# A hybrid decoder block on one core: the attention stage issued from a schedule made inside the kernel, with the last query tile and the first output products moved to the fourth and fifth query blocks

## The chip, the core and the metric

One core of one Trainium2 chip runs the whole kernel in one launch. The metric is the device time of an execution in microseconds (us). Before the change it is 1889.48 us, the median of three runs (1889.11 to 1890.73). The engines are named as in the profile: PE (TensorE, matrix products), PEld (its weight loads, which run beside the products), DVE (VectorE), ACT (ScalarE), POOL (GpSimd) and SP (SyncE, which here issues DMA transfers). "SPq" is the instruction queue of SP. Each engine takes its instructions strictly in the order in which they stand in its own program.

## The reference, cut to what matters

The block computes, on 1024 tokens of width 1024 in float32, a feed-forward part, a mixer and a second feed-forward part, each added to the running rows:

```python
h = h + 0.5 * swiglu(rms_norm(h, ffn1_norm[l]), ffn1_w_gu[l], ffn1_w_down[l])
h = h + hybrid_mixer(rms_norm(h, mix_norm[l]), w_in[l], ...)
h = h + 0.5 * swiglu(rms_norm(h, ffn2_norm[l]), ffn2_w_gu[l], ffn2_w_down[l])
return rms_norm(h, final_norm)
```

The change lies in the mixer. Half of its width is an attention of 8 query heads in 2 groups, with three branches that share the queries: compressed keys, selected key blocks and a window of 512 keys. With 16 blocks of 64 keys and 16 to be selected, every block is selected, so that the selected branch is plain causal attention. Each branch has its own softmax with a linear penalty on distance, and a gate from a sigmoid. The other half of the width is a gated linear recurrence, whose result is multiplied by a gate. Both halves together go through `w_out`.

## The kernel before

**Exact products from split operands.** Every float32 operand of a product is split into a high and a low part (`split`, lines 182 to 189: a copy on ACT or POOL, a subtraction on DVE), and `mm3` (lines 191 to 195) issues three products of 512 columns for one: high by high, high by low, low by high.

**The attention stage** (lines 1697 to 1768) runs from about 919 to 1249 us of the profiled execution. It goes over 8 blocks of 128 queries (`qb`), for each over the 2 groups (`g`), and for each group over its 4 heads (`hh`); `half` is 0 for the blocks 0 to 3 and 1 for 4 to 7. Below, (4,0) is block 4, group 0, and (4,0,2) its head 2. The steps of one head and one group are these:

- `att_soft`, lines 1261 to 1349: the scores of a head against the keys (`ka` high, `kl` low) are products on PE into a bank `a` (lines 1287 and 1288, 64 to 512 columns). DVE adds the distance table and finds the extreme (line 1295). The inner function `rest` then issues the exponentials on ACT (line 1333), the reciprocals of their sums on DVE (line 1336 for heads 0 and 1 together, line 1339 for heads 2 and 3) and the scaling on POOL (line 1345).
- `att_pv`, lines 1351 to 1396: for each block of keys, PE turns the four heads' probabilities with four transposes of 128 columns into a bank `b` (line 1376); ACT copies the high part `ph` (line 1378), DVE makes the low part `pt` (line 1379), and PE multiplies both with the values (line 1367) into the bank `o`. There are two banks `b`. The generator of one group is advanced while the scores of the next group are issued.
- Filling: a chain of generators `dense` is advanced between the heads. It holds work that is not attention: query projections (`att_proj_q`, lines 1181 to 1204; a tile of 128 columns of the query weights gives two heads and is 24 products of 512 columns), the gates of the recurrence (`late_gates`, lines 901 to 922: four times 24 products, a copy `ge` on ACT, and after the last one four sigmoids on ACT in a row) and, from block 4 on, the output product of the first 512 tokens (`wout`, lines 1399 to 1414).

**The filling before.** For the second half the query tiles go in the order 3, 0, the gates, then 1 and 2; at (3,1,2) the whole rest of that chain is issued, and only then the pool of the query weights is closed and the keys of the second half for group 0 are written (`att_kv`, lines 1237 to 1259, called in line 1722). Their high part `ka` lies in the buffer `wh` of the pool `wf`, which holds the weights of query tile 2 until that tile is done. The output product starts after the scores of (4,0): line 1745 makes its generator, and one step is issued at each head from (4,1) to (7,1), 28 steps in all. A step is half of a piece of 128 tokens by 256 columns: 12 products of 256 columns (lines 815 to 817). There are 16 pieces, so 32 steps; the last four are issued behind the last head (line 1750). Four pieces share one quarter of `w_out`, eight tiles of 256 KB (`wpages`, lines 370 to 380, tag `qa`, which the query heads use too). The step order within a piece is `kt` 0 to 3, which need the attention's result, then 4 to 7, which need the recurrence's result (lines 808 to 819). Behind the stage's last group, output products of the other 512 tokens (`rows_out`, lines 1757 to 1767; PE rows with `wq` as the moving operand and 512 columns) are issued between the parts of the last `att_pv`.

**What sets the order.** The code is written out as a straight program; the tile framework orders the instructions of every engine by the order of writing and by its own estimate of when each can start. `ordered` (lines 161 to 175) is a context that instead fixes, on each engine, the order in which the instructions were issued inside it. It is used at the kernel's start, and within `late_gates` for the four sigmoids. The attention stage as a whole is not in such a context.

## Time and profile before

| what | value |
|---|---|
| runs | 1889.11, 1889.48, 1890.73 us |
| profiled execution | 1889.76 us, its span 1888.0 us |
| PE, DVE, ACT, POOL busy in the span | 1863.8, 1348.6, 795.0, 535.0 us |
| granted TensorE clock | 0.999 |
| attention stage, first to last transpose | 934.9 to 1243.9 us |
| transposes, value products, output products of lines 815 to 817 with `wq` | 592, 296, 384 |
| ACT table loads, each 1283 ns | 9 in the program, 3 of them in the attention stage |

The page lists the busy time of each engine; a second view gives it by stretches of the span, a third the waits of one engine on another, and the timeline shows instructions in order of time. A PE product is counted busy from its start to a modelled end, so the products of a dense stream overlap: a product of 512 columns counts 0.38 us and the next one starts 0.21 to 0.22 us after it. A PE that counts as busy can therefore still be held up for a short while.

### The profile page before, as it was taken

What the parts mean: (1) busy time and instruction counts of PE and PEld (TensorE: products, weight loads), DVE (VectorE), ACT (ScalarE), POOL (GpSimd) and SP (SyncE); (2) the same over time, 40 slices, a digit from 0 to 9 for tenths busy, and PEclk for the clock granted to TensorE, in tenths of its full rate; (3) what the DMA queues carried; (4) which work ended last, traced back from release to release, by engine and by line L of the source; (5) the groups of instructions that cost most, each with busy time, mean ns of one, the idle gap of its engine ahead of it and who ended that gap; (6) DMA issues with size and microseconds to landing.
All of it is one profiled execution on the core that took longest, in us unless ns stands there. A gap on an engine that the chain in (4) does not pass through costs nothing.

```text
span 1888.0 us, 31252 instructions
## 1 busy us (share of the span) xinstructions
PE 1863.8 (99%) x11054; PEld 1620.8 (86%) x11054; DVE 1348.6 (71%) x2595; ACT 795.0 (42%) x1675; POOL 535.0 (28%) x641
## 2 busy tenths in 40 slices
PE   9999999999999999999999999999999999999998
PEld 6888888888888888889887888888888888888887
DVE  5988878657776545777477988737877776568686
ACT  5533333323323413334578777646333333323233
POOL 3132332324442001112345543311212222123222
PEclk9999999999999999999999999999999999999999
DMA  5246666428775232554522022553556675158664
GB/s 201 97 137 225 221 216 225 138 99 320 234 252 173 81 104 100 185 190 151 167 90 68 18 88 73 171 196 112 163 172 220 221 234 190 62 202 285 201 211 154
DMA packets 167260, 313.75 MB, mean 166 GB/s; under 512 B 17952, under 2 KB 50752, under 8 KB 167104
## 3 DMA queue, kind: packets, MB, share of 16 engines
q1 hardware_dynamic: 157568, 295.22, 47.2%
q10 hardware_dynamic: 9536, 16.53, 2.5%
q8 instruction: 87, 1.43, 0.3%
q14 instruction: 69, 0.57, 0.1%
HBM read 218.89 MB, written 92.80 MB: 165 GB/s over the span
## 4 chain that ended last, share of the span: by engine, by line
PE 87%; DVE 7%; ACT 3%; issue 2%; DMA 1%; POOL 1%; SPq 0%; POOLq 0%; ACTq 0%; DVEq 0%
PE b L193 18%; PE b L195 18%; PE b L194 18%; PE b L746 6%; PE b L744 6%; PE b L745 6%; PE b L1376 3%; PE b L1367 2%; PE b L969 1%; PE b L815 1%; ACT P L1333 1%; PE b L817 1%; PE b L816 1%; PE b L1288 1%; ACT ph L1378 1%
## 5 line engine op out<-in xcount | busy, mean ns | idle before, releaser
L193 PE MATMUL b<-xT,wp 128*128 128x512 f32 x1196 | 454.3, 380 | 1.7 <-DVE pd L696 1.3
L194 PE MATMUL b<-xT,wp 128*128 128x512 f32 x1196 | 453.8, 379 | 1.7 <-DVE xT L433 1.6
L195 PE MATMUL b<-xT,wp 128*128 128x512 f32 x1196 | 453.3, 379 | 0.0
L189 DVE TENSOR_TENSOR dw<-dr,dw 128x512 fp32r<-128x512 f32 x308 | 227.6, 788 | 62.1 <-ACT dw L187 51.0
L193 PEld LDWEIGHTS b<-xT,wp 128*128 128x128 f32 x1196 | 226.1, 189 | 37.0 <-DVE pd L696 1.7
L194 PEld LDWEIGHTS b<-xT,wp 128*128 128x128 f32 x1196 | 226.1, 189 | 35.4 <-DVE xT L433 3.5
L195 PEld LDWEIGHTS b<-xT,wp 128*128 128x128 f32 x1196 | 226.1, 189 | 32.7 <-DVE wp L189 0.3
L744 PE MATMUL b<-dw,dw 128*128 128x512 f32 x616 | 233.8, 380 | 0.3 <-DVE dw L189 0.3
L746 PE MATMUL b<-dw,dw 128*128 128x512 f32 x616 | 233.9, 380 | 0.0
L745 PE MATMUL b<-dw,dw 128*128 128x512 f32 x616 | 233.5, 379 | 0.0
L185 POOL TENSOR_SCALAR dw<-dr 128x512 fp32r<-128x512 f32 x154 | 127.2, 834 | 242.3 <-PE b L746 109.4
L187 ACT ACTIVATE wp<-ws 128x512 fp32r<-128x512 f32 x148 | 92.9, 629 | 235.5 <-PE b L194 226.1
L1345 POOL TENSOR_SCALAR P<-P,sm,gate 128x64 f32<-128x64 f32 (+8 forms) x192 | 126.8, 678 | 151.4 <-DVE sm L1336 54.0
L187 ACT ACTIVATE dw<-dr 128x512 fp32r<-128x512 f32 x154 | 91.8, 624 | 181.8 <-PE b L744 80.8
L189 DVE TENSOR_TENSOR wp<-ws,wp 128x512 fp32r<-128x512 f32 x148 | 113.8, 770 | 32.3 <-ACT wp L187 32.1
L187 ACT ACTIVATE wp<-wr 128x512 fp32r<-128x512 f32 x115 | 72.0, 627 | 145.7 <-PE b L194 120.8
L746 PEld LDWEIGHTS b<-dw,dw 128*128 128x128 f32 x616 | 116.4, 189 | 17.4 <-DVE dw L189 1.0
L744 PEld LDWEIGHTS b<-dw,dw 128*128 128x128 f32 x616 | 116.4, 189 | 17.2 <-issue 0.7
L745 PEld LDWEIGHTS b<-dw,dw 128*128 128x128 f32 x616 | 116.4, 189 | 16.3
L1333 ACT ACTIVATE P<-P,sm 128x64 f32<-128x64 f32 (+7 forms) x192 | 114.9, 600 | 35.4 <-DVE sm L1295 34.5
L529 POOL TENSOR_TENSOR ws<-wr 128x512 f32<-128x512 f32 x37 | 52.1, 1408 | 270.5 <-DVE wp L189 226.2
L193 PE MATMUL b<-xT,wh 128*128 128x512 f32 x320 | 125.8, 394 | 1.6 <-issue 1.4
(316 smaller groups left out, 3563.5 us busy)
## 6 DMA issues: line engine op xcount, KB each, us to landing
dr<-hs SPq DMA_DIRECT2D x242, 256.0 KB, 3.7
wr<-in_ffn_w_gu_dram SPq DMA_DIRECT2D x82, 512.0 KB, 4.2
hs<-hk SPq DMA_DIRECT2D x140, 256.0 KB, 4.0
hs<-wd SPq DMA_DIRECT2D x88, 256.0 KB, 3.1
wd<-in_ffn_w_down_dram SPq DMA_DIRECT2D x84, 256.0 KB, 3.4
dr<-in_ffn_w_down_dram SPq DMA_DIRECT2D x62, 256.0 KB, 4.4
wq<-wo SPq DMA_DIRECT2D x44, 256.0 KB, 3.3
wo<-wo SPq DMA_DIRECT2D x16, 512.0 KB, 2.7
```

The lines of the kernel that those rows point to most:

```text
L185: nc.gpsimd.tensor_scalar(out=hi, in0=src, scalar1=1.0, scalar2=1.0, op0=OP.mult, op1=OP.mult)
L187: nc.scalar.activation(out=hi, in_=src, func=AF.Copy)
L189: eng.tensor_tensor(out=lo, in0=src, in1=hi.bitcast(F32), op=OP.subtract)
L193: mm(ps, wh, xh, start=first, stop=False, skip_group_check=skip)
L194: mm(ps, wh, xl, start=False, stop=False, skip_group_check=skip)
L195: mm(ps, wl, xh, start=False, stop=last, skip_group_check=skip)
L744: mm(bs[t][:], hl[:, c], dh, start=first, stop=False, skip_group_check=True)
L745: mm(bs[t][:], hh[:, c], dh, start=False, stop=False, skip_group_check=True)
L746: mm(bs[t][:], hh[:, c], dl, start=False, stop=last, skip_group_check=True)
L1333: nc.scalar.activation(out=rng[br], in_=rng[br], func=AF.Exp, scale=-1.0, bias=m, accum_out=st[:, 6 + br:7 + br])
L1345: nc.gpsimd.tensor_scalar(out=rng[br], in0=rng[br], scalar1=st[:, 6 + br:7 + br], scalar2=self.gate[:, qb, h * 3 + br:h * 3 + br + 1], op0 ...
L1376: nc.tensor.transpose(b[:w, hh * 128:hh * 128 + 128], Ps[hh][i][:, c:c + w], self.ident[:])
```

## The change

**A planner.** A new class `Plan` stands in for the instruction builder inside a context `planned`. Calls to the five engines are recorded with the tiles that they read and write. `issue` then makes a schedule: it walks through time, keeps for each engine when it is free, for each operation when its inputs are ready, and for each tag when a buffer or a bank comes free, and takes next the operation that can start first, the earliest written one among equals. Durations come from formulas in `cost`. The operations are then issued for real in the order of their planned start, inside `ordered`, so that the order on every engine is the plan's. A function of ACT other than a copy carries its name, and a change of that function adds a table load of 1283 ns to the start that the plan sees. The whole loop of the attention stage, and what is written behind it up to the end of the last `att_pv`, goes through the plan. `flush("wq")` issues the plan up to the last operation that uses the pool of the query weights, so that the pool can be closed; the rest is planned again with that beginning held.

**The filling.** Query tile 2 of the second half leaves the chain that is used up at (3,1,2) and becomes a chain of its own: two steps at each of the heads (3,1,2) and (3,1,3), two at (4,0,0), three at (4,0,1), and what is left at (4,0,2). There the output product now starts, with two steps at each of the heads (4,0,2) and (4,0,3), then one at each head up to (7,1): 4 and 28, which is all 32. Within a piece the step with `kt` 4 to 7 now comes first.

**Buffers.** The keys of the second half for group 0 (`ka` and `kl`) lie in the pool `k1`, those for group 1 in the pool `wf`, in the buffers `wh` and `wl` of the query weights. In the first half, query tile 3 uses the bank `w` and not `b`, and in the second half tile 3 uses `b` and not `w`.

No instruction of the computation is added or left out. The program of ACT has 11 table loads in place of 9. The change moves all rows of the stage to line 208, the line in `issue` that calls the recorded operation.

The core of the diff:

```diff
+class Plan:
+    def cost(self, e, what, kw, out):
+        n = math.prod(out.shape[1:])
+        if e == "PE":
+            slot = max(109, n / 2.4 + 2.7)
+            return slot + 163, slot
+        if e == "ACT":
+            d = 173 + n * 0.83 + (103 if "accum_out" in kw else 0)
+            return d, d - 104, str(kw["func"]) if kw.get("func") != AF.Copy else None
+        if e == "DVE":
+            d = 145 + n * 1.06 + (70 if "accum_out" in kw else 0)
+            return d, d - 85
+        if e == "POOL":
+            d = 330 + n * 0.85
+            return d, d - 25
+        return 3500, 60
...
+    def issue(self, pool=None):
...
+            for e, ks in waiting.items() if best is None else ():
+                for k in ks:
+                    t = open_at(k)
+                    if t is not None:
+                        t = max(t, free[e]) + self.load(k, table)
+                        if best is None or (t, self.rank[k]) < best[:2]:
+                            best = t, self.rank[k], k, e
...
+            stall = (48 if self.ops[k][1] == "transpose" else 104) if e == "PE" and t > free[e] + 40 else 0
+            start[k], end[k], free[e] = t, t + dur, t + slot + stall
...
+        order = self.sent + sorted(order[len(self.sent):], key=lambda k: (start[k], k))
...
+        for k in order[len(self.sent):]:
+            self.ops[k][2](*self.ops[k][3], **self.ops[k][4])
...
+    @contextmanager
+    def planned(self):
+        nc, self.nc = self.nc, Plan(self.nc)
+        yield
+        self.flush()
+        self.nc = nc
+    def flush(self, pool=None):
+        plan, self.nc = self.nc, self.nc.nc
+        with self.ordered():
+            plan.issue(pool)
+        self.nc = plan
...
-        for kt in range(KT):
+        for z, kt in enumerate((4, 5, 6, 7, 0, 1, 2, 3)):
...
-                      net.att_proj_q(qp, turn, X, 1, "w", (1, 2)))
+                      net.att_proj_q(qp, turn, X, 1, "w", (1,)))
...
+        with net.planned():
...
+                            if (qb, g, hh) == (3, 1, 2):
+                                for _ in dense:
+                                    pass
+                                net.flush("wq")
+                                cv.close()
+                                kp1 = pool(cv, "k1", "right")
+                                net.att_kv(kp1, 1, (0,), bufs=1)
+                            if (qb, g, hh) == (3, 1, 2):
+                                dense = net.att_proj_q(qp, turn, X, 1, "w", (2,))
+                            if (qb, g, hh) == (4, 0, 2):
+                                for _ in dense:
+                                    pass
+                                for i in range(2):
+                                    m_tiles(2 + i, 0)
+                                    net.split(M[0][2 + i][0][:], M[1][2 + i][0][:], mohg[i, 0][:])
+                                dense = net.wout(sp2, M, 0, hspill)
...
-                        for _ in range(1 if half else (4, 4, 2, 2, 2, 2, 3, 2)[qb * 2 + g]):
+                            for _ in range((2, 3, 2, 2)[hh] if (qb, g) == (4, 0) else 1 if half else 2 if (qb, g, hh // 2) == (3, 1, 1) else (4, 4, 2, 2, 2, 2, 3, 2)[qb * 2 + g]):
```

**Three places in the programs.** In the rows below, `ka`, `kl`, `kch` and `kcl` are key tiles and `qa` a query head (scores), `P` a head's probabilities and `ident` the identity (transposes), `ph`, `pt` and `vhl` the operands of the value products, `xT` with `wh` or `wl` a query projection, `wq` with `xT` the output product. The number behind a name tells one tile from another.

The first place is PE at the scores of head (4,0,1) and the first transposes of the group before. Before, the rows are these:

```order
L1287 MATMUL b_10948<-ka_10778,qa_9765 128x128
L1288 MATMUL b_10948<-kl_10779,qa_9765 128x128
L1287 MATMUL b_10952<-kch,qa_9765 128x64
L1288 MATMUL b_10952<-kcl,qa_9765 128x64
L1376 MATMUL b_10957<-ident,P_10671 128x128
L1376 MATMUL b_10957<-ident,P_10787 128x128 x2
L1376 MATMUL b_10966<-ident,P_10671 128x128 x2
L1376 MATMUL b_10966<-ident,P_10787 128x128 x2
L1287 MATMUL b_10997<-ka_9378,qa_10575 128x512
L1288 MATMUL b_10997<-kl_9379,qa_10575 128x512
L817 MATMUL b_11191<-wq_11173,xT_9618 128x256
```

Now query tile 2 (bank 10622) stands between the last scores of that head, on the same engine:

```order
L208 MATMUL b_10660<-ka_10614,qa_9536 128x128
L208 MATMUL b_10660<-kl_10615,qa_9536 128x128
L208 MATMUL b_10622<-xT_5707,wh_9702 128x512
L208 MATMUL b_10661<-kch,qa_9536 128x64
L208 MATMUL b_10661<-kcl,qa_9536 128x64
L208 MATMUL b_10622<-xT_5708,wh_9702 128x512
L208 MATMUL b_10622<-xT_5707,wl_9703 128x512
```

Twelve products of that tile stand between the scores of (4,0,0) and the transposes behind (4,0,1), where no filling stood; and 48 products with `wq` follow before the scores of (4,1,0), where there were 7.

The second place is ACT at the sigmoids of the gates (`ge`), with the exponentials (`P`) before and behind. Before, they stand ahead of the exponentials of head (2,1,3):

```order
L913 ACTIVATE ge_10409<-b_10291 128x512
L919 ACT_TABLE_LOAD
L919 ACTIVATE ge_9911<-ge_9911 128x512
L919 ACTIVATE ge_10064<-ge_10064 128x512
L919 ACTIVATE ge_10230<-ge_10230 128x512
L919 ACTIVATE ge_10409<-ge_10409 128x512
L1378 ACTIVATE ph_10425<-b_10420 128x512
L1378 ACTIVATE ph_10434<-b_10429 128x512
L1333 ACT_TABLE_LOAD
L1333 ACTIVATE P_1845_10393,sm_10348<-P_1845_10393,sm_10348 128x64
```

Now three sigmoids stand five heads earlier, ahead of the exponentials of (2,0,2), with a table load ahead and one behind:

```order
L208 ACT_TABLE_LOAD
L208 ACTIVATE ge_9570<-ge_9570 128x512
L208 ACTIVATE ph_9638<-b_9637 128x512
L208 ACTIVATE ge_9605<-ge_9605 128x512
L208 ACTIVATE ge_9643<-b_9621 128x512
L208 ACTIVATE ph_9645<-b_9644 128x512
L208 ACTIVATE ge_9643<-ge_9643 128x512
L208 ACTIVATE ph_9648<-b_9647 128x512
L208 ACT_TABLE_LOAD
L208 ACTIVATE P_1797_9633,sm_9634<-P_1797_9633,sm_9634 128x384
```

And the fourth stands alone further on, between the exponentials of (3,0,0) and (3,0,1):

```order
L208 ACTIVATE P_1859_9695,sm_9696<-P_1859_9695,sm_9696 128x64
L208 ACTIVATE ot_9700<-b_9663 64x512
L208 ACT_TABLE_LOAD
L208 ACTIVATE ge_9684<-ge_9684 128x512
L208 ACT_TABLE_LOAD
L208 ACTIVATE P_1869_9705,sm_9696<-P_1869_9705,sm_9696 128x512
```

The four sigmoids thus have two pairs of table loads in place of one.

The third place is PE at the scores of head (7,0,2), where the first value product of the group before, (6,1), needs a `ph` from ACT. Before:

```order
L1287 MATMUL b_12823<-ka_9378,qa_10575 128x192
L1288 MATMUL b_12823<-kl_9379,qa_10575 128x192
L1287 MATMUL b_12827<-ka_10778,qa_10575 128x512
L1367 MATMUL b_12769<-ph_12775,vhl 128x512
L1288 MATMUL b_12827<-kl_10779,qa_10575 128x512
L1287 MATMUL b_12831<-ka_9378,qa_10575 128x512
L1288 MATMUL b_12831<-kl_9379,qa_10575 128x512
```

Now, on the same engine:

```order
L208 MATMUL b_11125<-ka_9378,qa_9722 128x192
L208 MATMUL b_11125<-kl_9379,qa_9722 128x192
L208 MATMUL b_11126<-ka_10614,qa_9722 128x512
L208 MATMUL b_11126<-kl_10615,qa_9722 128x512
L208 MATMUL b_11127<-ka_9378,qa_9722 128x512
L208 MATMUL b_11127<-kl_9379,qa_9722 128x512
L208 MATMUL b_11128<-ka_10614,qa_9722 128x512
L208 MATMUL b_11109<-ph_11111,vhl 128x512
```

The value product stands behind seven score products of that head, where it stood behind three. Over blocks 5 to 7 the PE programs otherwise read much alike.

More of the change, by code (lines that the diff above doesn't have):

```diff
@@ L1186, in att_proj_q @@
             w = wp(i)
-            b = self.bank(tag if tag != "ba" else "ba"[m])
+            b = self.bank(tag if len(tag) == 1 else tag[m])
             for kt in range(KT):
@@ L1235, in att_tables, with att_kv @@
                                 pattern=[[0, 8]], base=-31, channel_multiplier=1, compare_op=OP.is_ge, fill=0.0)
[L1237 removed]
+    def att_kv(self, p, half, gs=(0, 1), tags=("ka", "kl"), bufs=2):
         nc = self.nc
@@ L1244, in att_kv @@
             pb, other = slice(g * 64, g * 64 + 64), slice(64 - g * 64, 128 - g * 64)
[L1245 to L1247 removed]
+            ka = self.KA[g, half] = p.tile([128, W], F32R, name=self.nm("ka"), tag=tags[0], bufs=bufs)
+            kl = self.KL[g, half] = p.tile([128, W], F32R, name=self.nm("kl"), tag=tags[1], bufs=bufs)
             nc.gpsimd.memset(kl[other].bitcast(F32), 0.0)
@@ L1748, in body @@
-        for _ in old:
-            pass
-        for _ in dense:
-            pass
-        w = [net.wrows(0, (4, 5, 6, 7, 0, 1), net.wq_tile), None]
-        for kp in (2, 3):
-            m_tiles(kp, 1)
-            net.split(M[0][kp][1][:], M[1][kp][1][:], mohg[kp - 2, 1][:], "act")
-        def rows_out(bs, c, kts, first, last, tts=range(4)):
-            for kt in kts:
-                for i in tts:
-                    x = [M[k][kt // 2][1][:, kt % 2, i * 128:i * 128 + 128] for k in range(2)]
-                    net.mm3(bs[i][:], *x, *w[c][kt], kt == first, kt == last)
@@ L1763, in body, with rows_out @@
-        bs = [net.bank() for _ in range(4)]
-        for kt in range(4, 8):
-            next(pv)
-            rows_out(bs, 0, (kt,), 4, 3)
-        for _ in pv:
-            pass
+        with net.planned():
+            pv = old = None
+            raw = {}
+            for half in range(2):
+                for qb in range(4 * half, 4 * half + 4):
+                    for g in range(2):
+                        if qb == 4 and g:
+                            net.att_kv(wf, 1, (1,), ("wh", "wl"), 1)
+                        Ps = []
+                        for hh in range(4):
+                            if (qb, g, hh) == (3, 1, 2):
[14 more added lines that the diff above has]
+                                dense = net.wout(sp2, M, 0, hspill)
+                            *P, rest = net.att_soft(sp2, g, qb, hh)
+                            Ps.append(P)
+                            for _ in old or ():
+                                pass
+                            for _ in range((2, 3, 2, 2)[hh] if (qb, g) == (4, 0) else 1 if half else 2 if (qb, g, hh // 2) == (3, 1, 1) else (4, 4, 2, 2, 2, 2, 3, 2)[qb * 2 + g]):
+                                if next(dense, None):
+                                    break
+                            if pv and hh:
+                                next(pv, None)
+                                if hh == 1:
+                                    next(pv, None)
+                                if hh == 3:
+                                    next(pv, None)
+                            rest()
+                        old = pv
+                        if (g, half) not in raw:
+                            if half == 0:
+                                m_tiles(g, 0)
+                            raw[g, half] = half and mop.tile([128, 2, 512], F32, name=f"ao{g}", tag="mo", bufs=4)
+                        pv = net.att_pv(sp2, g, qb, Ps, raw[g, half], None if half else [M[hl][g][0] for hl in range(2)])
+            for _ in old:
+                pass
+            for _ in dense:
+                pass
+            w = [net.wrows(0, (4, 5, 6, 7, 0, 1), net.wq_tile), None]
+            for kp in (2, 3):
+                m_tiles(kp, 1)
+                net.split(M[0][kp][1][:], M[1][kp][1][:], mohg[kp - 2, 1][:], "act")
+            def rows_out(bs, c, kts, first, last, tts=range(4)):
+                for kt in kts:
+                    for i in tts:
+                        x = [M[k][kt // 2][1][:, kt % 2, i * 128:i * 128 + 128] for k in range(2)]
+                        net.mm3(bs[i][:], *x, *w[c][kt], kt == first, kt == last)
+            bs = [net.bank() for _ in range(4)]
+            for kt in range(4, 8):
+                next(pv)
+                rows_out(bs, 0, (kt,), 4, 3)
+            for _ in pv:
+                pass
```

194 lines of the change are left out of this document (148 added, 46 removed).

## The prediction

> **What bounds the kernel now.** I read the page first: the busy time of each engine over the span, and the granted clock.
>
> ```profile
> span 1888.0 us, 31252 instructions
> PE 1863.8 (99%) x11054; PEld 1620.8 (86%) x11054; DVE 1348.6 (71%) x2595; ACT 795.0 (42%) x1675; POOL 535.0 (28%) x641
> PEld 6888888888888888889887888888888888888887
> PEclk9999999999999999999999999999999999999999
> ```
>
> PE is the bound, at the full clock, and counts as idle for only 24 us in all. The second view is the busy time by stretches of the attention stage. I cut out 1018 to 1062, the neighbourhood of the 22nd slice (991 to 1038), where PEld falls to 7 tenths, and the end behind the last scaling at 1212.
>
> ```profile
> 919.00:940.00 21.00, 19.50 (x107) 17.19 (x106) 11.73 (x62) 14.56 (x53) 7.51 (x19) 1.00 0.33 101
> 940.00:1018.00 78.00, 76.40 (x421) 65.94 (x421) 55.29 (x197) 61.10 (x179) 43.87 (x77) 1.00 0.27 85
> 1018.00:1040.00 22.00, 19.70 (x117) 15.57 (x116) 18.23 (x55) 19.62 (x47) 8.77 (x14) 1.00 0.12 38
> 1040.00:1062.00 22.00, 20.61 (x124) 16.37 (x124) 21.25 (x66) 15.87 (x42) 13.73 (x16) 1.00 0.00 1
> 1062.00:1212.00 150.00, 145.17 (x996) 129.72 (x996) 123.90 (x387) 107.65 (x243) 61.74 (x82) 1.00 0.28 85
> 1212.00:1249.00 37.00, 36.91 (x222) 31.42 (x221) 19.75 (x35) 15.60 (x30) 3.23 (x3) 1.00 0.33 110
> sum 330.00, PE 318.29 PEld 276.22 DVE 250.16 ACT 234.39 POOL 138.86; mean PE 53.05 PEld 46.04 DVE 41.69 ACT 39.07 POOL 23.14
> ```
>
> Behind the length stand the busy times of PE, PEld, DVE, ACT and POOL. Half of the kernel's idle PE time lies here: 330 - 318.3 = 11.7 us. Idle time is not all of it. In the timeline of PE a product of 512 columns counts 0.38 us and lets the next start after 0.22; behind a wait it is 0.32; one of 256 columns takes 0.11:
>
> ```profile
> 1050.98 0.38 PE L1367 MATMUL b<-pt,vhl 128*128 128x512 f32 x1
> 1051.20 0.38 PE L1367 MATMUL b<-ph,vhl 128*128 128x512 f32 x1
> 1051.83 0.48 PE L1367 MATMUL b<-pt,vhl 128*128 128x512 f32 x1 [0.26 <-DVE pt L1379]
> 1052.15 0.38 PE L1367 MATMUL b<-ph,vcm 128*128 128x512 f32 x1
> 1053.08 0.28 PE L816 MATMUL b<-wq,xT 128*128 128x256 f32 x1
> 1053.19 0.28 PE L817 MATMUL b<-wq,xT 128*128 128x256 f32 x1
> ```
>
> So short hold-ups hide under the busy time. As a measure that sees them I take the share of PEld, since every product has one weight load: 0.85 in 940 to 1018 and 1212 to 1249, 0.86 in 1062 to 1212, but (15.57 + 16.37) / 44 = 0.73 in 1018 to 1062. As dense as the stretch before it, those 31.94 us of loads would need 37.8 us: 6.2 us are lost there. The waits of PE in 919 to 1249 say on whom:
>
> ```profile
> PE b L1367 <- ACT ph L1378: 4.4, 7, 1.0
> PE b L1376 <- DVE pt L1379: 3.1, 7, 0.6
> PE b L193 <- issue: 1.4, 1, 1.4
> PE b L1288 <- DVE kl L1259: 0.6, 1, 0.6
> ```
>
> PE waits for the split of the turned probabilities. It is not that ACT and DVE are full over the stage (234 and 250 of 330 us), but that PE has nothing else in its queue at that point.
>
> **The change part by part.** The sum is made against the profiled execution, 1889.76 us, which is 0.28 above the median; the instructions are the same but for two table loads, so it can only come from PE's lost time and from new waits.
>
> (a) 1018 to 1062. Four steps of the output product, 48 products at 0.11 us (the rows at 1053.08 and 1053.19), come here from behind the last head: 5.3 us of PE work is put where 6.2 us are lost. It costs nothing that it leaves the end: in 1212 to 1249 DVE and ACT are busy for 19.75 and 15.60 us, so even if 5.3 us go from the 37 they are at 0.62 and 0.49, and the products of `rows_out` still cover the last group. The keys of group 0 no longer stand behind query tile 2, so the 0.6 us wait for `kl` should go as well. Against it stands that tile 2 itself, 24 products at 0.22 = 5.2 us, leaves the time just before 1018 for this one. DVE sets a floor: 18.23 + 21.25 = 39.5 of the 44 us, so the stretch itself cannot get much shorter; the gain is that the later work is done in it. I take 5.3; the bounds are 0 (DVE has the say, and holes open in block 3) and 7.1 (the density of 1062 to 1212: 31.94 / 0.865 = 36.9).
>
> (b) 1062 to 1212. The order reads much alike, and the gain is in the detail. At the scores of head (7,0,2) this is PE, then ACT, then DVE:
>
> ```profile
> 1172.02 0.40 PE L1287 MATMUL b<-ka,qa 128*128 128x512 f32 x1
> 1173.45 0.48 PE L1367 MATMUL b<-ph,vhl 128*128 128x512 f32 x1 [1.03 <-ACT ph L1378]
> ```
>
> ```profile
> 1171.53 1.15 ACT L1333 ACTIVATE P<-P,sm 128x1024 f32<-128x1024 f32 x1 [0.59 <-DVE sm L1295]
> 1172.80 1.09 ACT L1378 ACTIVATE ph<-b 128x512 fp32r<-128x512 f32 x2
> ```
>
> ```profile
> 1172.81 0.19 DVE L1336 RECIPROCAL sm<-sm 128x6 f32<-128x6 f32 x1 [0.97 <-ACT P L1333]
> ```
>
> The copy `ph` stands behind a long exponential; PE has the rest of the scores queued behind the value product that needs it. Now four more score products, 4 x 0.22 = 0.9 us, stand ahead of that product, so of 1.0 us nearly all is covered, as long as ACT does not come later. How much of this the planner finds over the whole stretch I bound by density. The best slices in and near it are these:
>
> ```profile
> 970.00:980.00 10.00, 10.00 (x60) 9.03 (x59) 7.25 (x27) 7.88 (x25) 4.78 (x9) 1.00 0.11 18
> 1120.00:1130.00 10.00, 9.49 (x73) 9.11 (x73) 8.85 (x32) 8.02 (x19) 3.69 (x5) 1.00 0.14 41
> 1200.00:1210.00 10.00, 9.92 (x71) 9.01 (x69) 8.25 (x26) 7.70 (x17) 5.37 (x8) 1.00 0.30 71
> ```
>
> At 0.906, the mean of the last two, 129.72 us of loads would need 143.2 in place of 150: 6.8 us at most; nothing at least. I take half, 3.4: a schedule by durations should remove waits of half a microsecond, and cannot remove those in which DVE is 8 to 9 tenths busy.
>
> (c) 940 to 1018. At 0.88, between its own 0.845 and the 0.90 of 970 to 980, the 65.94 us would need 74.9: 3.1 us at most. I take half, 1.5. Against it stand the two table loads:
>
> ```profile
> 994.18 1.28 ACT L919 ACT_TABLE_LOAD   x1
> 995.48 2.19 ACT L919 ACTIVATE ge<-ge 128x512 f32<-128x512 f32 x4
> 998.66 1.28 ACT L1333 ACT_TABLE_LOAD   x1
> 999.95 0.35 ACT L1333 ACTIVATE P<-P,sm 128x64 f32<-128x64 f32 x1
> ```
>
> From the start of the load to the start of the next instruction is 1.30 us, so ACT loses 2.6 us more. Queued behind the new pair are the exponentials of (3,0,1), for which POOL's scaling and then the transposes wait. ACT is busy for 61.10 of the 78 us and PE has query products to do, so I charge 0.5; the bounds are 0 and 2.6. (The Trainium skill, "ScalarE: Activation LUTs", section "What ACT_TABLE_LOAD costs", speaks against this part of the change: a switch is 1283 ns and a drain of some 1380 ns, 2.66 us in all. The trace agrees on the 1283 and shows no drain. By the page ACT would lose 5.3 us, and charged in the same proportion PE would lose 1.0 in place of 0.5, by estimate.) The multiplications of the gates on POOL also come earlier, ahead of scalings; POOL is busy for 43.87 of 78 us and in no row above does PE wait for it: nothing, at most the 1.4 us that I take as gain.
>
> (d) 919 to 940. One wait is most of its 1.5 us:
>
> ```profile
> 938.45 0.45 PE L193 MATMUL b<-xT,wh 128*128 128x512 f32 x1 [1.43 <-issue]
> ```
>
> It is the first product with the weights of query tile 3, whose load is issued ahead of the planned part, and whose place on PE has not moved: no gain, and no loss.
>
> (e) SP. The page loads of the output product now stand among the loads and stores of `res`, where they stood in rows of seven or eight. Taken at nothing while the work between two quarters covers them; the price without that cover is the last rival's.
>
> Sum: 5.3 + 3.4 + 1.5 - 0.5 = 9.7 us; 1889.76 - 9.7 = 1880.1 for a profiled execution, and 0.3 less, 1879.8, for the median.
>
> **The rivals.** *Only the moved filling counts.* The order of blocks 5 to 7 reads alike because the framework's own estimate was already good, and b and c give nothing: 5.3 us, 1884.2. For it: the PE rows; against it: the wait at 1173.45, which the new row order answers.
>
> *The plan also takes the hidden hold-ups.* All at their upper bounds: 7.1 + 6.8 + 3.1 = 17 us, 1872.5. For it: every wait avoided also spares the 0.1 us between 0.22 and 0.32. Against it: DVE at 21.25 of 22 us in 1040 to 1062.
>
> *The filling only changes places.* Tile 2 leaves block 3, holes of up to its 5.2 us open there, as ACT and DVE go on at their pace; with the table loads' 2.6 that is 7.8 us, and it eats the 5.3 together with half of what (b) and (c) are forecast to bring, 2.5. Time 1889.5, no change. For it: ACT busy for 19.62 of 22 us in 1018 to 1040. Against it: before 1018 ACT is at 0.78 and DVE at 0.71, so the transposes there need less cover.
>
> *The pages come late: slower.* A quarter of `w_out` is eight loads into tiles of the quarter before. Their order is still `kt` 0 to 7, but the first step now needs `kt` 4 to 7, the last four, which can only start when the last step of the quarter before has left their tiles. In that place SP, and then the time from issue to landing (least, median, most), are now:
>
> ```profile
> 1084.69 7.05 SPq L377 DMA_DIRECT2D wq<-wo  x7
> 1092.54 0.39 SPq L377 DMA_DIRECT2D wq<-wo  x1
> DMA to landing us min/median/max: 2.6/3.3/5.4
> ```
>
> By the order, the work on PE between the last product of the first quarter and the first of the second is 20 transposes (0.11), 12 value products (0.22) and 8 score products (1.3 together): 6.1 us. Two issues at 0.39 and the median landing are 4.1, so it is covered. If the eight loads are strung out over 7 us as in the row, PE, which cannot pass a product that waits, stands for 7.05 + 3.3 - 6.1 = 4.3 to 7.05 + 5.4 - 6.1 = 6.3 us at each of three changes: 13 to 19 us, 1892.7 to 1898.8, in the middle 1895.7. It decides from the point at which the first page lands over 6.1 us behind the last step. Against it: the 7 us arise since each load waits for a tile, and four of the eight now start a step earlier.
>
> **How the numbers follow.** Chances: the forecast 0.48, only the filling 0.18, the hidden hold-ups too 0.10, only changed places 0.12, late pages 0.12. The first three are faster by over 0.2% (3.8 us, about what a measurement of this kernel can tell from no change): 0.76; the fourth is within it, 0.12; the last slower, 0.12. The time is the likeliest case's, 1879.8. The range goes from 1870, a little under the sum of all upper bounds, to 1889, which leaves out the late pages and half of the changed places, 0.18.
>
> **What would show it.** Right: PEld's share in the stretch of (3,1) to (4,1) rises from 0.73 to over 0.80; the stage ends 8 to 12 us earlier and everything behind it is only shifted; the wait of 1.03 us at (7,0,2) falls under 0.4. The table loads cost something if the transposes of (2,1) and (3,0) wait for POOL or ACT. Wrong: PE waits for a DMA at the first output product of a quarter; a lower share of PEld in block 3 than the 0.845 of now; or a stage as long as before with ACT and DVE less busy.

## The result and the profile after

The changed kernel takes 1874.45 us, the median of six runs (1872.38 to 1874.73), beside 1889.76 us for the kernel before on the same chip. The ratio is 0.9916, with a 95% interval of 0.9903 to 0.9929: 15 us faster, where 9.7 were forecast. The profiled execution took 1874.73 us, its span is 1873.0 us, 15.0 under that of before. From its page:

```profile
PE 1855.4 (99%) x11054; PEld 1621.2 (87%) x11054; DVE 1346.1 (72%) x2595; ACT 796.6 (43%) x1677; POOL 536.0 (29%) x641
PEld 6888888888888888889888999888888888888887
```

The instructions of every engine are as many as before, but for the two table loads of ACT. The 7 in the middle of PEld's line is gone, and three slices of the stage stand at 9. The busy time by stretches, with the columns as before (length, PE, PEld, DVE, ACT, POOL, clock, DMA):

```profile
919.00:940.00 21.00, 21.00 (x116) 18.63 (x115) 10.99 (x54) 13.69 (x50) 7.46 (x18) 1.00 0.33 99
940.00:1018.00 78.00, 75.86 (x426) 65.58 (x425) 58.88 (x212) 69.57 (x195) 43.79 (x77) 1.00 0.31 99
1018.00:1040.00 22.00, 20.87 (x131) 18.08 (x130) 19.91 (x57) 17.59 (x45) 13.14 (x18) 1.00 0.01 2
1040.00:1062.00 22.00, 22.00 (x169) 20.98 (x168) 19.28 (x69) 15.42 (x38) 12.75 (x17) 1.00 0.14 43
1062.00:1197.00 135.00, 133.62 (x938) 122.78 (x936) 114.26 (x364) 100.18 (x231) 57.21 (x76) 1.00 0.30 91
1197.00:1234.00 37.00, 36.83 (x215) 31.20 (x214) 24.08 (x45) 20.17 (x38) 4.16 (x5) 1.00 0.29 100
sum 315.00, PE 310.18 PEld 277.25 DVE 247.41 ACT 236.62 POOL 138.51; mean PE 51.70 PEld 46.21 DVE 41.23 ACT 39.44 POOL 23.09
```

The stage's work is the same (PEld 277.25 us, before 276.22) and needs 315 us in place of 330. PE is idle for 315 - 310.2 = 4.8 us, before 11.7. PEld's share in 1018 to 1062 is (18.08 + 20.98) / 44 = 0.89, before 0.73; in 1062 to 1197 it is 0.91, before 0.86. What PE waits for in 919 to 1234 (total, times, longest):

```profile
PE b L208 <- ACT ph L208: 1.5, 4, 0.5
PE b L208 <- DVE pt L208: 1.5, 4, 0.6
PE b L208 <- DVE qa L208: 0.5, 1, 0.5
PE b L208 <- POOL P L208: 0.4, 1, 0.4
```

Before, PE waited 8.1 us for `ph` and `pt` in 919 to 1249, with the 4.4 and 3.1 of the prediction's rows and this one:

```profile
PE b L1367 <- DVE pt L1379: 0.6, 2, 0.3
```

Now it is 3.0 us, and no wait is for a DMA. At head (7,0,2), where PE waited 1.03 us, its timeline (start, busy) now reads:

```profile
1166.82 0.38 PE L208 MATMUL b<-ka,qa 128*128 128x512 f32 x1
1167.34 0.48 PE L208 MATMUL b<-ph,vhl 128*128 128x512 f32 x1
```

From the last score product to the value product it is 0.52 us, before 1.43. A dense stream has 0.22, so 0.30 us are lost in place of 1.21.

**Where the 15 us came from.** To sum such losses, waits and hidden hold-ups alike, I took for each group the time from its first transpose to that of the next group, and subtracted PE's products in it, each at the step of a dense stream: 0.216 us for 512 columns, 0.109 for 256 columns and for a transpose, 0.083 for 128 and 0.060 for 64 (the other widths at steps between). What remains is PE's lost time. It doesn't depend on which filling stands in the group, but time that products lose by running at half the granted clock is in it. Before and after, the clock was full throughout the stage; it was at half for some 3.4 us of the stage in e1 and in e6, 6.8 in e12, 10 in e11 and 37 in e3. In us:

| kernel | blocks 0 to 2 | (3,0) to (4,0) | (4,1) to (7,1) | whole stage |
|---|---|---|---|---|
| before | 7.0 | 12.0 | 13.0 | 32.9 |
| after | 5.4 | 5.1 | 5.9 | 17.3 |
| gained | 1.6 | 6.9 | 7.1 | 15.6 |
| e1, plan with the old filling | 5.8 | 11.5 | 5.0 | 22.9 |
| e2, new filling without the plan | 5.7 | 11.2 | 12.3 | 30.1 |
| e3, durations x 0.6 | 26.4 | 27.2 | 49.6 | 104.1 |
| e11, durations x 0.9 | 15.2 | 11.1 | 17.8 | 44.9 |
| e12, durations x 1.1 | 2.8 | 8.7 | 2.6 | 14.9 |
| e6, durations x 1.3 | 2.5 | 10.5 | 13.6 | 27.2 |
| e5, table load at 1800 ns | 7.5 | 11.6 | 5.8 | 25.6 |
| e9, the same, way back at once | 6.9 | 5.3 | 5.9 | 18.9 |

(The last column has up to 1.0 us more, from ahead of the first and behind the last transpose.) The first transpose of (3,0) came at 1020.0 and comes at 1013.2, that of (7,0) at 1196.1 and 1188.1, and the last one of all at 1243.9 and 1228.7. (Behind (6,1) part of the shift is output products that left.)

### The profile page after: what moved, and what is told of

It reads as the page before. It is cut to its first block, busy times and chain, and to the rows that moved or that the text cites. A ratio compares the mean times of both kernels' runs of the same rounds, so it can differ in the third digit from the quotient of the medians.

```text
span 1873.0 us, 31240 instructions
## 1 busy us (share of the span) xinstructions
PE 1855.4 (99%) x11054; PEld 1621.2 (87%) x11054; DVE 1346.1 (72%) x2595; ACT 796.6 (43%) x1677; POOL 536.0 (29%) x641
## 3 DMA queue, kind: packets, MB, share of 16 engines
q8 instruction: 87, 1.43, 0.3%
## 4 chain that ended last, share of the span: by engine, by line
PE 88%; DVE 6%; ACT 2%; DMA 2%; issue 1%; SPq 0%; POOL 0%; POOLq 0%; DVEq 0%; ACTq 0%
PE b L394 17%; PE b L396 17%; PE b L395 17%; PE b L208 13%; PE b L945 6%; PE b L947 6%; PE b L946 6%; PE b L1170 1%; DVE dw L390 1%; ACT P L208 1%; PE b L1327 1%; DVE xf L639 1%; PE b L455 1%; DVE wp L390 1%; DMA dr<-hs 1%
## 5 line engine op out<-in xcount | busy, mean ns | idle before, releaser
L947 PEld LDWEIGHTS b<-dw,dw 128*128 128x128 f32 x616 | 116.4, 189 | 17.3 <-DVE dw L390 0.7
L208 ACT ACTIVATE P<-P,sm 128x640 f32<-128x640 f32 (+8 forms) x192 | 114.7, 600 | 33.6 <-DVE sm L208 33.3
L208 DVE TENSOR_TENSOR pt<-b,ph 128x512 fp32r<-128x512 f32 x148 | 98.6, 687 | 24.6 <-ACT ph L208 23.7
```

The costliest lines, as they stand in the source:

```text
L208: self.ops[k][2](*self.ops[k][3], **self.ops[k][4])
L947: mm(bs[t][:], hh[:, c], dl, start=False, stop=last, skip_group_check=True)
```

## The experiments

Three theories stood at the start. O: the planner's order brings the larger part by itself. F: nearly all comes from the moved filling. B: neither brings much without the other. The later runs ask what the planner's numbers are worth. Each kernel's time is a median, and each ratio is against the kernel before on the same chip.

**e1: the plan with the old filling.** Buffers and banks are as in the changed kernel.

```diff
-        for z, kt in enumerate((4, 5, 6, 7, 0, 1, 2, 3)):
+        for z, kt in enumerate(range(KT)):
...
-                      net.att_proj_q(qp, turn, X, 1, "w", (1,)))
+                      net.att_proj_q(qp, turn, X, 1, "w", (1, 2)))
...
-                            for _ in range((2, 3, 2, 2)[hh] if (qb, g) == (4, 0) else 1 if half else 2 if (qb, g, hh // 2) == (3, 1, 1) else (4, 4, 2, 2, 2, 2, 3, 2)[qb * 2 + g]):
+                            for _ in range(1 if half else (4, 4, 2, 2, 2, 2, 3, 2)[qb * 2 + g]):
```

(The output product is made after the scores of (4,0) again.)

> The planner, the new banks and the new key buffers, but the filling as before the change: query tile 2 in the chain that is used up at (3,1,2), the output product only behind the scores of (4,0), its steps with kt 0 to 7 in that order. After the change the median is 1874.45 us, before 1889.76. Theory O (the planner's order by durations gives the larger part, the moved filling some 5 to 7 us): 1879.5 to 1882. Theory F (the moved filling is nearly all, the planner reproduces an order that was already good): 1886 or more. Theory B (neither works without the other, since the planner needs work that it may move): about 1884 to 1888.

Measured: 1880.3 us (1878.77 to 1881.11), ratio 0.995 (0.9934 to 0.9967), some 9.6 us faster than before. Its stretch from 1018 to 1062:

```profile
1018.00:1062.00 44.00, 39.08 (x245) 33.38 (x244) 39.37 (x127) 34.15 (x84) 24.33 (x34) 0.96 0.05 16
```

PEld's share there is 33.38 / 44 = 0.76, hardly above the 0.73 of before, and the table gives 11.5 us lost around it. But what PE waits for has changed (919 to 1240), and a part of (4,0) ran at half the clock:

```profile
PE b L208 <- DVE sm L208: 2.9, 3, 1.8
PE b L208 <- DVE pt L208: 1.9, 4, 0.7
PE b L208 <- ACT ph L208: 1.6, 4, 0.6
```

```profile
1050.00:1053.50 3.50, 1.03 (x9) 0.69 (x7) 2.80 (x7) 1.65 (x4) 1.86 (x2) 1.00 0.00 0
1053.50:1057.00 3.50, 3.50 (x13) 3.00 (x13) 3.46 (x14) 2.05 (x6) 0.41 (x1) 0.51 0.00 0
```

The plan alone takes the waits for `ph` and `pt` from 8.1 to 3.5 us. In (4,0) PE now waits for DVE at the scores, and the 3.4 us at half the clock behind that are worth up to 1.7 of the 11.5 us. In blocks (4,1) to (7,1) the plan alone takes all that the change takes: 13.0 to 5.0.

**e2: the new filling without the plan.** The instructions go to the framework in the order of writing.

```diff
     def planned(self):
-        nc, self.nc = self.nc, Plan(self.nc)
         yield
-        self.flush()
-        self.nc = nc
...
     def flush(self, pool=None):
-        plan, self.nc = self.nc, self.nc.nc
-        with self.ordered():
-            plan.issue(pool)
-        self.nc = plan
+        return
```

> The moved filling, the new banks and the new key buffers, without the planner: the tile framework sets the order from the new writing. Theory O: the 5.3 us of moved products and the 1.4 us wait for the bank w are gained, the rest is not: 1882 to 1884. Theory F: 1875 to 1878. Theory B: 1886 to 1890.

Measured: 1886.23 us (1884.77 to 1888.09), ratio 0.9978 (0.9968 to 0.9987), 3.7 us faster. The same stretch, then PE's waits in 919 to 1249:

```profile
1018.00:1062.00 44.00, 40.05 (x261) 34.63 (x260) 35.73 (x111) 30.60 (x76) 21.77 (x29) 1.00 0.06 20
```

```profile
PE b L1561 <- ACT ph L1572: 4.4, 7, 1.0
PE b L1570 <- DVE pt L1573: 3.9, 10, 1.0
PE b L1561 <- DVE pt L1573: 0.3, 1, 0.3
```

The waits for `ph` and `pt` are those of before (8.6, before 8.1), although 48 more output products now stand close by. So F falls. Over the stage the larger part is the plan's, as O has it: 9.6 of 15.3 us in e1, 3.7 in e2 (which lies in B's band, 2.2 us above O's). The new banks and key buffers are in both, though, and no run is without them alone; the banks are worth 1.0 to 1.6 us by group (0,0) (see e4). So the filling alone brings some 2 us, and what only both together bring is 15.3 - 9.6 - 3.7 = 2.0 and the banks' share that was taken off twice, 3.0 to 3.6, less up to 1.7 for the clock in e1. In (3,0) to (4,0) it is clearly B: the plan alone takes 0.5 us there (at most 2.2 without the clock drop) and the filling alone 0.8, both together 6.9. Filling helps only where it stands in PE's queue ahead of the product that has to wait. A plan can only put it there if it may come so early: in (3,0) and (3,1), e1 has 9 output products and 3 query products, the changed kernel 72 and 23. Whether the place in the writing or the new step order (`kt` 4 to 7 first) allows that, no run separates.

**e4: the old banks for query tiles 0, 2 and 3.** Only the strings of banks go back.

```diff
-        dense = chain(net.att_proj_q(qp, turn, X, 0, "bw", (2, 3)),
-                      net.att_proj_q(qp, turn, X, 1, "b", (3,)),
-                      net.att_proj_q(qp, turn, X, 1, "w", (0,)),
+        dense = chain(net.att_proj_q(qp, turn, X, 0, "b", (2, 3)),
+                      net.att_proj_q(qp, turn, X, 1, "w", (3, 0)),
```

> After the change, but the query tiles use the banks of before: tiles 2 and 3 of the first half bank b, tiles 3 and 0 of the second half bank w. If the wait of 1.43 us at 938.45 before was for the single bank w, as the same place without a wait after the change suggests: it comes back, 1875.5 to 1876.5. If it was for a weight load, as the prediction put it: no change, 1874.2 to 1874.7.

Measured: 1874.85 us (1873.95 to 1875.81), ratio 0.992 (0.9905 to 0.9935): between the two expectations, and not to be told from the changed kernel. In the timeline of PE the wait of 938.45 comes back in part (brackets: idle before, releaser):

```profile
936.80 0.67 PE L208 MATMUL b<-xT,wh 128*128 128x512 f32 x2 [0.36 <-issue]
```

In the changed kernel a product of the same tile goes without a wait:

```profile
936.18 0.62 PE L208 MATMUL b<-xT,wh 128*128 128x512 f32 x2
```

Group (0,0) loses 2.04 us with the old banks and 1.06 with the new; in e2, with the new banks and no plan, it loses some 0.6, before 2.2. So it was the banks: before, tiles 3 and 0 of the second half went to the single bank `w` one after the other, and the second had to wait until the first was read out. The plan hides part of it with a value product ahead of the wait.

**e3: ACT and DVE planned too short.**

```diff
-            d = 173 + n * 0.83 + (103 if "accum_out" in kw else 0)
+            d = 0.6 * (173 + n * 0.83 + (103 if "accum_out" in kw else 0))
...
-            d = 145 + n * 1.06 + (70 if "accum_out" in kw else 0)
+            d = 0.6 * (145 + n * 1.06 + (70 if "accum_out" in kw else 0))
```

> After the change, but the planner's durations of ACT and DVE are 0.6 of what they were; all else is the same, the computation too. Theory O in its strict form (it is the true durations that place products ahead of waits): the planner believes that split parts are ready sooner, and PE stands again before value products and transposes: 1879 to 1885, with waits of PE on ph and pt of 8 us or more in the stage in place of 3. If only the freedom to reorder matters and not the durations: 1874 to 1877.

Measured: 1961.69 us (1959.44 to 1962.3), ratio 1.0377 (1.0362 to 1.0393): 87 us slower than the changed kernel, far outside both expectations. PE's waits in 919 to 1320, since this stage ends at 1314:

```profile
PE b L208 <- DVE pt L208: 42.3, 35, 4.6
PE b L208 <- ACT ph L208: 12.1, 6, 3.3
PE b L208 <- DVE sm L208: 8.5, 8, 2.8
```

The plan believes `pt` to be ready and sets the value product directly behind the transposes. Since the order is fixed, PE can't take anything else in the meantime. These waits are 62.9 of the 87 us; part of the rest may be the clock's (see the last section).

**e6: ACT and DVE planned too long.** The same edit with 1.3 in place of 0.6.

> After the change, but the planner's durations of ACT and DVE are 1.3 of what they were. With 0.6 of them the time was 1961.7 us. If only durations that are too short do harm (the planner then puts PE behind results that are not there, while with too long ones it puts more other work ahead): 1873 to 1880. If any error of this size does harm, since the order across ACT and DVE goes wrong too: 1885 to 1930.

Measured: 1882.94 us (1880.87 to 1883.53), ratio 0.9962 (0.9949 to 0.9976): 8.5 us slower than the changed kernel, between the two expectations. Three tenths too long cost a tenth of what four tenths too short cost. The loss stands in single groups. In (5,0) and (6,0) the plan has 7.9 us of filling each, in (4,1) and (5,1) 2.6 each, where the changed kernel has 5.2 in all four; (5,0) and (6,0) lose 3.1 and 4.9 us, in the changed kernel 0.4 and 1.0. Part of it is a wait that PE has in no other run, for the pages of `w_out` (919 to 1240):

```profile
PE b L208 <- DMA wq<-wo: 3.0, 6, 1.0
```

Of it 1.1 us are in (5,0) and 1.6 in (6,0): pages do come late where a plan bunches the filling. In (6,0) the clock was also at half for 3.4 us, worth up to 1.7. How much of the rest comes from the place of the filling is not shown.

**e11 and e12: a tenth less, a tenth more.** The same edit with 0.9 and with 1.1.

> Durations of ACT and DVE times 0.9 in the planner. Theory L (the cost of a short duration grows with the shortage): a quarter of the 87 us at 0.6, some 22 us, 1890 to 1900. Theory T (there is a margin; only when the plan asks for more of ACT and DVE than they can give does the loss open): within 4 us of the changed kernel, 1873 to 1878.5; a third pair of table loads is in it, for at most 1.5 us of that.

> Durations of ACT and DVE times 1.1. Theory L: a third of the 8.5 us at 1.3, 2.8 us, 1876 to 1878.5. Theory T: a margin on this side too, and the filling stands where it stood, 1873 to 1875.5. If the sigmoids in one group with the way back three instructions later cost what they cost with the charge of 1800 ns: 1880 to 1884.

Measured for 0.9: 1899.88 us (1899.17 to 1902.47), ratio 1.0055 (1.0043 to 1.0068), slower than the kernel before. For 1.1: 1870.8 us (1869.75 to 1871.02), ratio 0.9897 (0.9883 to 0.991). This is the fastest version by its median, though not surely below the changed kernel: the intervals of the two ratios overlap, but the slowest of its four runs is 1.4 us under the fastest of the six of the changed kernel, although the kernel before was no faster beside it (1890.15 us). On the short side it was theory L: 25 us, where a quarter of 87 is 22. On the long side all three expectations failed, since none foresaw a gain. PE's waits for `pt` and `ph` in 919 to 1240, with 0.9 and then with 1.1:

```profile
PE b L208 <- DVE pt L208: 9.4, 13, 3.1
PE b L208 <- ACT ph L208: 8.0, 10, 1.4
```

```profile
PE b L208 <- DVE pt L208: 0.4, 1, 0.4
PE b L208 <- ACT ph L208: 0.4, 1, 0.4
```

That is 17.4 us, 3.0 in the changed kernel and 0.8. From 1.0 to 1.1 the two waits fall by 2.2 us, about all of the 2.4 by which the lost time falls. From 0.9 to 1.0 they are 14.4 of 27.6 us; the half clock is worth up to 5 more, and the rest is not assigned. The number of table loads differs too (three pairs of loads around sigmoids with 0.9, one with 1.1, two in the changed kernel), which by e9 and e10 matters little. The formulas themselves were not short. For 512 columns they give 173 + 425 = 598 ns on ACT and 145 + 543 = 688 on DVE, and the changed kernel's groups (total, mean ns of one) show:

```profile
L208 ACT ACTIVATE ph<-b 128x512 fp32r<-128x512 f32 x148 | 85.2, 593 | 31.4 <-PE b L208 29.6
L208 DVE TENSOR_TENSOR pt<-b,ph 128x512 fp32r<-128x512 f32 x148 | 98.6, 687 | 24.6 <-ACT ph L208 23.7
```

So a plan with the right durations is not the best one. What delays the chain besides them, I did not measure.

**e5: the table load dearer in the plan.** The intention was that the four sigmoids go together again.

```diff
-        return 1283 if mine and mine[0] and table and mine[0] != table else 0
+        return 1800 if mine and mine[0] and table and mine[0] != table else 0
```

> After the change, but the planner charges 1800 ns in place of 1283 for a change of the table on ACT; the four sigmoids then stand together in block 3 with one pair of loads (9 loads in the program in place of 11). If the two extra loads cost what the lost PE time of the first heads of block 2 suggests (3.1 us in (2,0) and (2,1) in place of 2.3 before the change): 1873.4 to 1874.0. If ACT's 2.6 us lie under the query products: no change, 1874.2 to 1874.7.

Measured: 1882.38 us (1881.43 to 1886.59), ratio 0.9967 (0.9955 to 0.998). The sigmoids go together, two loads are saved, and the kernel is 7.9 us slower than the changed one, against both expectations. The timeline of ACT:

```profile
995.00 0.33 ACT L208 ACTIVATE P<-P,sm 128x64 f32<-128x64 f32 x1
...
996.08 1.28 ACT L208 ACT_TABLE_LOAD   x1
997.37 2.19 ACT L208 ACTIVATE ge<-ge 128x512 f32<-128x512 f32 x4
1000.44 1.08 ACT L208 ACTIVATE ph<-b 128x512 fp32r<-128x512 f32 x2 [0.88 <-PE b L208]
1002.99 2.57 ACT L208 ACTIVATE ka<-kr 64x512 fp32r<-64x512 f32 x4 [1.46 <-PE b L208]
...
1009.70 1.20 ACT L208 ACTIVATE ph<-b 128x512 fp32r<-128x512 f32 x2 [1.80 <-PE b L208]
1012.47 0.60 ACT L208 ACTIVATE ph<-b 128x512 fp32r<-128x512 f32 x1 [1.58 <-PE b L208]
1013.09 1.28 ACT L208 ACT_TABLE_LOAD   x1
1014.38 0.72 ACT L208 ACTIVATE P<-P,sm 128x512 f32<-128x512 f32 x1
```

Between 995.24 and 1014.38 there is no exponential, and ACT stands idle for 5.7 us of it, waiting for PE. The planner takes what can start first. After the sigmoids every exponential carries the charge, so a copy that can only start up to 1.8 us later is still taken ahead of it; the longest of the idle times is 1.80. Then 18 exponentials follow with one copy among them, up to 1025.59, and PE is idle for a quarter of the time; the stretch 1020 to 1040, in this kernel and in the changed one:

```profile
1020.00:1040.00 20.00, 15.21 (x87) 11.15 (x85) 15.14 (x34) 17.72 (x45) 14.04 (x23) 1.00 0.00 1
```

```profile
1020.00:1040.00 20.00, 18.87 (x117) 16.30 (x116) 18.10 (x53) 15.80 (x40) 12.46 (x18) 1.00 0.00 1
```

**e9 and e10: the way back at once.** That reading is tested by charging the way back to the exponentials in the plan's times, but not in the choice. The way to a sigmoid costs 1800 ns in e9 and 1283 in e10.

```diff
-    def load(self, k, table):
+    def load(self, k, table, choice=False):
         mine = self.ops[k][7][2:]
-        return 1283 if mine and mine[0] and table and mine[0] != table else 0
+        if not (mine and mine[0] and table and mine[0] != table):
+            return 0
+        return (1800 if mine[0] == str(AF.Sigmoid) else 0) if choice else 1283
...
-                        t = max(t, free[e]) + self.load(k, table)
+                        t = max(t, free[e]) + self.load(k, table, True)
...
             t, _, k, e = best
+            if len(order) >= len(self.sent):
+                t += self.load(k, table) - self.load(k, table, True)
```

> The four sigmoids stand together at the same place as with the charge of 1800 ns, with one pair of table loads, but when the planner compares starts it charges nothing for the way back to the exponentials, so that their load follows the last sigmoid at once; the planned start still has the 1283 ns. Theory W (the loss of 7.9 us with the charge of 1800 ns came from the way back: any copy could start earlier than an exponential with the charge on it, so ACT held the exponentials from 995.24 to 1014.38 us and stood idle for some 5.7 us of that): the loss goes, 1872.5 to 1876. Theory G (grouping itself costs it: sigmoids and gates come late, whatever stands behind): the loss stays, 1880 to 1884.

> As the run before, with 1283 ns charged on the way to a sigmoid: one sigmoid alone early, the other three together later, two pairs of table loads as in the changed kernel. Theory W: as the changed kernel within 1.5 us, 1873 to 1876. Theory G: three of four sigmoids late, 1877 to 1883.

Measured: e9 1876.31 us (1876.09 to 1877.32), ratio 0.9928 (0.9915 to 0.9942); e10 1874.94 us (1874.61 to 1875.71), ratio 0.9921 (0.9907 to 0.9934). The sigmoids of e9 stand at the same place as in e5, and the load follows at once:

```profile
1000.11 2.19 ACT L212 ACTIVATE ge<-ge 128x512 f32<-128x512 f32 x4
1002.32 1.28 ACT L212 ACT_TABLE_LOAD   x1
1003.62 0.73 ACT L212 ACTIVATE P<-P,sm 128x512 f32<-128x512 f32 x1
```

Of the 7.9 us 6.1 are gone, nearly all of it in (3,0) to (4,0), 11.6 to 5.3 lost: theory W, though e9 lies 0.3 us above its band. The 1.9 us that stay above the changed kernel, not certain by the intervals of the ratios, are in blocks 0 to 2 (6.9 lost against 5.4), so some of G may be left. One pair of loads (e9) is no faster than two (e10).

**e7 and e8: two edits without an effect that shows.** In e7 the planner's cost of POOL is nearer to the trace; in e8 the pages with `kt` 4 to 7 are loaded first, since they are used first.

```diff
-            d = 330 + n * 0.85
+            d = 360 + n * 0.93
```

> After the change, but the planner's duration of POOL is 360 + 0.93 n in place of 330 + 0.85 n, by the rows of before (412 ns for 64, 950 for 640 columns against 384 and 874 by the formula). In the profile after, PE waits for POOL once, 0.4 us. If that is all: 1874.0 to 1874.5; if POOL's formula shifts the order of the exponentials and transposes: up to 2 us to either side.

```diff
-        for kp in range(4):
+        for kp in (2, 3, 0, 1):
...
+        h, l = h[4:] + h[:4], l[4:] + l[:4]
```

> After the change, but the eight loads of a quarter of w_out are issued in the order in which its first piece now uses them (kt 4 to 7, then 0 to 3). If the late pages of the prediction's slower rival cost anything now, 0.5 to 2 us less: 1872.5 to 1874. If they are covered, as the profile after shows no wait of PE for a DMA: no change, 1874.2 to 1874.7.

Measured: 1874.04 us (1872.4 to 1875.07), ratio 0.9916 (0.9903 to 0.993), and 1873.96 us (1872.01 to 1874.11), ratio 0.9914 (0.9901 to 0.9928). Neither is to be told from the changed kernel's time. The order of the pages costs nothing here that these runs can tell.

## Why the prediction was right in direction and too small

The result lies in the range, near the second rival (1872.5): the plan also takes the hidden hold-ups. That rival's mechanism came nearest to what happened, and it had a chance of only 0.10; the range held because it reached down to the upper bounds. (The terms below are compared with groups, which only roughly match the stretches of the forecast.)

- **(a) 1018 to 1062.** Forecast 5.3, lost time fell by 6.9 in (3,0) to (4,0), inside the bounds (0 to 7.1). That the size was near is partly luck, since the reason was only half right. The text credits it to 48 output products put into holes; e2 puts them there and gains 0.8. It needs the plan as well. The argument against, that DVE with 39.5 of 44 us has the say, did not hold: DVE did the same there, 19.91 + 19.28 = 39.2 us, while PEld's work rose from 31.94 to 39.06.
- **(b) 1062 to 1212.** This is the term that was mis-sized: forecast 3.4, measured 7.1 in (4,1) to (7,1), a little above the bound of 6.8. The bound came from the densest slices of the kernel, and half of it was taken since a plan "cannot remove those in which DVE is 8 to 9 tenths busy". It could: DVE is busy for 114.26 of 135 us there now, 0.85, PEld's share is 0.91, and e12 takes another 3.3 us. An engine that was busy 0.85 of the time was no bound here, with its work ordered so that PE hardly waits for it. The mechanism was right: e1 shows that the plan alone does this part, and the wait at (7,0,2) went as foretold.
- **(c) 940 to 1018.** Forecast 1.5 - 0.5 = 1.0. From (0,1) to (2,1) lost time fell from 4.8 to 4.3, so 0.5. In (2,0) and (2,1), where the sigmoids now stand, it rose from 2.3 to 3.1, 0.8 more, within the bounds of the table loads' price. But the loads are not shown to be its cause: e9 has one pair and loses 3.9 there, e10 two and 3.3, e12 one and 1.6. Nor is it that query tile 2 left (2,1): e1 keeps it there and loses 3.5. From a load to the next instruction it is 1.30 us, as before (e9's rows at 1002.32 and 1003.62). The cause stays open.
- **(d) 919 to 940.** This step failed. The text took the wait of 1.43 us for that of a weight load and expected no gain. It was the bank `w`, in which tile 3 no longer precedes tile 0; group (0,0) lost 2.2 us and loses 1.1. The product is not the first with the weights of tile 3, as the text says, but of tile 0: it is the 73rd query product of the stage, a tile has 24, and the order is 2 and 3 of the first half, then 3 and 0 of the second. "issue" in the row only says that the profile saw no releaser; a weight load was a guess.
- **(e) SP.** Right: PE waits for no DMA, and loading the pages in the order of use (e8) gains nothing. The rival of late pages is out for this plan; e6, which bunches the filling, shows it at 3.0 us.

So the sum 5.3 + 3.4 + 1.0 + 0 = 9.7 stands against 6.9 + 7.1 + 0.5 + 1.1 = 15.6 (the span: 15.0; the rest of the kernel differs by 0.6). Of the 5.9 us missed, 3.7 are the halving in (b). One sum of the rivals was wrong as well: with changed places, 5.3 + 3.4 + 1.5 - 7.8 leaves a gain of 2.4 us, so some 1887 in place of 1889.5.

Of the marks, PEld's share rose above 0.80 (0.89), the wait at (7,0,2) fell under 0.4 (the gap is 1167.34 - 1167.20 = 0.14), and the last transpose comes 15.2 us earlier, above the 8 to 12. One mark of "wrong" is touched by a hair: PEld's share in 940 to 1018 is 65.58 / 78 = 0.841, before 0.845. It was badly chosen, because part of another group lies in that stretch now; the lost time by groups compares like with like.

## What to carry to other kernels

A fixed order is worth as much as the numbers behind it, and they should err on the long side: in this kernel a tenth too short cost 25 us, a tenth too long gained 3.6 (likely, but within the intervals), three tenths too long cost 8.5. Filling and the plan that places it belong together; judge neither alone. In a list scheduler that takes whatever can start first, a switching cost on the way back can hold off the work that everybody waits for: charged at 1800 ns it cost 6 us here (e5 against e9), while the 1283 ns of the changed kernel cost nothing that shows (e10).

## What the hardware showed beside that

The granted clock of TensorE fell to half in the profiled execution of e12, in the middle of busy work. Two stretches, then the products in them that PE had waited for (start, busy, idle before):

```profile
1030.00:1034.00 4.00, 2.41 (x10) 1.60 (x9) 3.91 (x13) 3.98 (x11) 2.59 (x3) 0.90 0.00 0
1034.00:1040.00 6.00, 5.69 (x22) 5.08 (x23) 5.87 (x12) 2.68 (x7) 4.27 (x4) 0.50 0.01 3
```

```profile
1031.04 0.48 PE L208 MATMUL b<-ka,qa 128*128 128x512 f32 x1 [0.95 <-DVE sm L208]
1032.48 0.48 PE L208 MATMUL b<-ph,vhl 128*128 128x512 f32 x1 [0.39 <-ACT ph L208]
1034.31 0.77 PE L208 MATMUL b<-wq,xT 128*128 128x256 f32 x2 [0.56 <-issue]
```

Up to 1030 the clock was full. PE was then idle for 4 - 2.41 = 1.6 of 4 us, never for more than 0.95 us at a time, and the clock fell to 0.50 near the end of that stretch (a mean of 0.90 over 4 us is 0.8 us at half) and stayed there up to 1040. (The 8.7 us of e12 in the table contain this.) The Trainium skill, "TensorE: Matmul & The Clock Gate", section "HAM oscillation — how this bites in real kernels", gives as the rule that PE should have no idle gaps over about 3.4 us. The trace shows the drop after far shorter ones; it is nearer to the Trainium skill's next section on that page, "A second HAM failure mode: psum-queue depth-cycling", in which frequent short idle times do it. They do not always do it: in the profiled execution of e5 PE was busy for 1.83 of 4 us, and the clock stayed full. What decides, no run here shows.

```profile
1005.00:1009.00 4.00, 1.83 (x9) 1.20 (x7) 2.11 (x4) 2.83 (x5) 0.00 (x0) 1.00 0.51 161
```

What the drops cost differs. In e12, two runs with a mean clock of 0.997 took 1870.75 and 1871.02 us, two with 0.999 took 1869.75 and 1870.85: at most about a microsecond, while DVE was busy for 5.87 of those 6 us. In e5 the same program took 1885.46 and 1886.59 us at 0.997, and 1881.43 to 1882.38 in its three other runs: about 4 us. That DVE was the bound in e12 would explain the difference, but the slower executions of e5 have no profile. In e3 the clock averaged 0.989, so that up to (0.999 - 0.989) x 1957.7 = 20 of its 87 us may be the clock's.
